# One operand sum of a Winograd-style matmul unit moved to a ScalarE negation and an adding DMA, with the products and the sums of h in another order (two-layer hybrid decoder trunk, 1 core)

## Chip, cores and metric

One core of one Trainium2 chip. The metric is the time of one execution in microseconds on the device; lower is better. Before the change three runs gave 2301.86, 2302.67 and 2303.2 us, median 2302.67 us.

## What is computed

A decoder trunk of two layers on 256 tokens of width 2048, everything in float32. Cut to its products, a layer is

```python
h = rms_norm(x, mix_norm[l])
z = h @ w_in[l]                                  # 2048 x 7168
a_out = chunked_spatial_gating(z[..., :c_a], ...)
b_out = dilated_attention(z[..., c_a:c_q], z[..., c_q:c_k], z[..., c_k:], ...)
mixed = concat(rms_norm(a_out), rms_norm(b_out))
x = x + mixed @ w_out[l]                         # 2048 x 2048
h = rms_norm(x, ffn_norm[l])
x = x + (silu(h @ w_gate[l]) * (h @ w_up[l])) @ w_down[l]   # 2048 x 5632, twice, and 5632 x 2048
```

The change concerns the last line, the FFN.

## The kernel before, in words

**Numbers.** Each float32 operand is split in two float32r halves, `hi` (a rounded copy, written by ScalarE) and `lo` (the rest, by a VectorE subtraction). A product is three matmuls, hi·hi, hi·lo and lo·hi (`mm3`, line 836). Weights arrive as raw tiles of 128 x 4 x 512 (1 MB) on SyncE's DMA queue and are split by `split_w`: ScalarE writes `wh`, then VectorE writes `wl = raw - wh`.

**Order.** The engines' queues are written out by hand. A list of items is walked; an item has a `prep` (load and split of its weights) and a `run` (its matmuls). Preps run ahead of runs by a ring of weight slots: 6 slots (`UNIT_RING`), two per item of four k-tiles, so the prep of item n+2 is issued just ahead of the run of item n. Other work, in generators called jobs, is issued between matmuls when a rough clock of each engine (`Queues`) says that it is due; `pause` and `Lease` belong to this planner. Nothing of the planner runs on the chip; it fixes the order in each queue, and semaphores do the rest.

**FFN stages.** In a layer the gate and up weights go by 11 column blocks j of 512, in chunks of 4, 4 and 3; after each chunk the down projection of that chunk follows, in two units (pairs of column blocks). One `unit` (line 871) multiplies the 256 tokens with two column blocks over some k-tiles by seven products instead of eight (the Strassen-Winograd form, `s` k-tiles per quarter: 4, or 2 in the last chunk's down units) and then adds plain products for the other k-tiles. Of the weights the quarters B11, B12, B22, B21 are loaded. `early` (line 890) makes e = B12 - B11 and overwrites B12 by B22 - B12, both on VectorE. `p1` makes B11 := B12 + B11 after splitting B11, `p2` makes B11 := B21 - B11 ahead of its split of B21. The items of a unit are, with the form of the activations that each takes: p1 (11), p5 (S1, weights e), p6 (S2, weights B11), p2 (12, weights B21), p7 (S3, weights B12), p3 (S4, weights B22), p4 (22, weights B11), then four plain items (`plains`). The runs r1 to r7 copy PSUM banks in between on ScalarE (after r1: X from bank 1; after r5: s5; after r6: Y from X; after r7: s3) and add s3 and s5 on VectorE after r3 and r4. `early` of the next unit stands behind the prep of the last plain item (five items earlier for the first unit).

**h.** At the end of a gate/up unit `gu_bank` (line 738) makes h on ScalarE and VectorE, pauses `H_NS` = 4000 ns of planner time and calls `put_h` (line 701): TensorE transposes, then for the first two blocks of a chunk the raw copy `xg` and, with the second, all seven forms by `make_forms` (line 619); for later blocks `quad_T` (line 258) splits straight into a plain table. The forms of the FFN input are made in the same way at the end of the attention stage (`put_f`), and the input of the next layer by `x_columns`.

Buffers of 8 KB per partition come from a pool of 22 (`SLOTS`).

Of the kernel before, what the change touches and what calls it, by code (L numbers as in the profile page):

```python
# [32 lines left out]
KC = 4  # L33
HK = 2
S_GU = 4
FORMS = ("11", "22", "S1", "S3", "S2", "12", "S4")

SLOTS = 22
PLAIN_RAW, PLAIN_RING = 3, 4
# [2 lines left out]

MM_NS = 227
FFN_LIMIT = 30000
H_NS = 4000
MARGIN_NS = 800
BACKLOG_NS = 4000
UNIT_NS = 3000
# [93 lines left out]
def trunk_kernel(ctx: ExitStack, tc: tile.TileContext, aps: dict):  # L142
# [21 lines left out]
    def slot(shape, dtype, name):  # L164

        return gen.tile(list(shape), dtype, tag="g", name=name)
# [33 lines left out]
    def pause(ns):  # L200
        q.chain = max(q.chain, q.pe) + ns
        yield


    class Job:
        def __init__(self, steps, limit):
# [48 lines left out]
                    identity=ident)  # L255
        return tp

    def quad_T(src_of, put, g_of, name, free=lambda: None):

        yield from sd_lease.take(2)  # L260
        both = slot([P, 2, 4, SEQ], F32R, name)
        hi, lo = both[:, 0], both[:, 1]
        tps = [transpose_pair(src_of, 2 * pr, name + "p") for pr in range(2)]
        free()
        yield
        for pr in range(2):
            tp = tps[pr]
            if g_of is None:
                sl = slice(2 * pr, 2 * pr + 2)
                act.activation(out=hi[:, sl, :], in_=tp, func=ACTF.Copy)  # L270
                dve.tensor_tensor(
                    out=lo[:, sl, :], in0=tp, in1=hi[:, sl, :].bitcast(F32), op=ALU.subtract)
            else:
                for i in range(2):
                    k = 2 * pr + i
                    split_scaled(hi[:, k, :], lo[:, k, :], tp[:, i, :], g_of(k))
            sd_lease.give()
            if pr == 0:
                yield
        put(hi, lo)  # L280

# [334 lines left out]
            sd_lease.give()  # L616
            yield

    def make_forms(F, xg):

        def quarter(t, h):
            return xg[:, h, :F.s, t * P:(t + 1) * P]
        a11, a12, a21, a22 = quarter(0, 0), quarter(0, 1), quarter(1, 0), quarter(1, 1)

        def split(f, src):
            hi, lo = F.at(f)
            act.activation(out=hi, in_=src, func=ACTF.Copy)
            dve.tensor_tensor(out=lo, in0=src, in1=hi.bitcast(F32), op=ALU.subtract)
            F.ready.add(f)
        split("11", a11)  # L630
        split("22", a22)
        dve.tensor_tensor(out=a22, in0=a21, in1=a22, op=ALU.add)
        dve.tensor_tensor(out=a21, in0=a11, in1=a21, op=ALU.subtract)
        yield
        split("S1", a22)
        split("12", a12)
        dve.tensor_tensor(out=a11, in0=a22, in1=a11, op=ALU.subtract)
        dve.tensor_tensor(out=a12, in0=a12, in1=a11, op=ALU.subtract)
        yield
        split("S2", a11)  # L640
        split("S3", a21)
        split("S4", a12)


    def x_columns(j, ssq, put, g_of, scale_done):
        cols = slice(j * W, (j + 1) * W)
        for t in range(NT):
            act.activation(
                out=junk, in_=xs[t][:, cols], func=ACTF.Square, accum_out=ssq[:, t, j:j + 1])
        yield from put(j, lambda t: xs[t][:, cols], lambda k: g_of(4 * j + k))  # L650
        if j == D // W - 1:
            scale_done()

    def put_plain(table, name):
# [4 lines left out]
    def put_f(L):  # L659

        plain = put_plain(L.fT, "fT")

        def put(j, src_of, g_of):
            if j >= 2:
                yield from plain(j, src_of, g_of)
                return
            if j == 0:
                L.xg = slot([P, 2, 4, SEQ], F32, "xg")
            yield from raw_T(src_of, L.xg[:, j], g_of, "fTp")
            if j == 1:  # L670
                L.f_halves = form_halves(8, "fF")
                L.fF = Forms(L.f_halves, S_GU)
                yield from make_forms(L.fF, L.xg)
        return put

    def wout_done(L, j, part):
# [17 lines left out]
    class Chunk:  # L694
# [4 lines left out]
            self.table, self.F, self.xg = {}, None, None  # L699

        def put_h(self, j, src_of, free):
            i = j - self.j0
            if i >= 2:
                yield from quad_T(
                    src_of, lambda hi, lo: self.table.__setitem__(i, (hi, lo)), None, "hT", free)
                return
            if i == 0:
                self.xg = slot([P, 2, 4, SEQ], F32, "xg")
            yield from raw_T(src_of, self.xg[:, i], None, "hTp", free)
            if i == 1:  # L710
                s = self.s
                if s < 4:
                    both = slot([P, 2, 2, 4 - s, SEQ], F32R, "hR")
                    rest = self.xg[:, :, s:, :]
                    for h in range(2):
                        act.activation(out=both[:, 0, h], in_=rest[:, h], func=ACTF.Copy)
                        dve.tensor_tensor(
                            out=both[:, 1, h], in0=rest[:, h], in1=both[:, 0, h].bitcast(F32),
                            op=ALU.subtract)
                    yield  # L720
                    flat = both.rearrange("p a h k t -> p a (h k) t")
                    self.table["r"] = (flat[:, 0], flat[:, 1])
                F = Forms(form_halves(6, "hF") + [self.L.f_halves[7]], s)
                self.F = F
                yield from make_forms(F, self.xg)

        def form(self, f, k):
            drain(lambda: self.F is not None)
# [9 lines left out]
    def gu_bank(L, j, chunk):  # L738

        s = {}  # L740

        def done(n, t, bank):
            if n == 0:
                yield lambda: hasattr(L, "r2")
                yield from t2_lease.take(1)
                s[t] = t2("s")
                act.activation(out=s[t], in_=bank, func=ACTF.Silu, scale=L.r2[:, t:t + 1])
                mm_lease.give()
                return
# [7 lines left out]
            yield from pause(H_NS)  # L757
            yield from chunk.put_h(j, lambda t: s[t], lambda: t2_lease.give(2))
        return done

# [110 lines left out]
    def unit(s, quarter, plains, form, done, lead=1):  # L871
# [16 lines left out]
            q.chain = saved  # L888

        def early():  # L890
            x11, x12, x22 = need(b11), need(b12), need(b22)
            U["e"] = slot([P, s, W], F32, "e")
            live[0] += 1
            w_sum(U["e"], x12, x11, ALU.subtract)
            w_sum(x12, x22, x12, ALU.subtract)

        def p1(it, parts=1):
            it.w = split_w(b11.tile)
            w_sum(b11.tile, b12.tile, b11.tile, ALU.add)

        def p5(it, parts=1):
            it.w = split_w(U["e"])
# [3 lines left out]
            it.w = split_w(b11.tile)  # L906

        def p2(it, parts=1):
            w_sum(b11.tile, need(b21), b11.tile, ALU.subtract)
            it.w = split_w(b21.tile)  # L910
            live[0] -= 1

        def p7(it, parts=1):
            it.w = split_w(b12.tile)
            live[0] -= 1

        def p3(it, parts=1):
            it.w = split_w(b22.tile)
# [37 lines left out]

        def r3(it):
            product(it, "S4", "Y", False)
            w_sum(bank["Z"], bank["Z"], U["s3"], ALU.add)

        def r4(it):
            product(it, "22", "X", False)
            w_sum(bank["Y"], bank["Y"], U["s5"], ALU.add)

        for p, r in ((p1, r1), (p5, r5), (p6, r6), (p2, r2), (p7, r7), (p3, r3), (p4, r4)):
            items.append(Item(1 if s <= 2 else 2, UNIT_RING, p, r))
        early_at[len(items) - 7 - lead] = early

        names = {(0, 0): "1", (1, 0): "Y", (0, 1): "X", (1, 1): "Z"}
        for i, (n, srcs, ops) in enumerate(plains):  # L970
            r = Raw(srcs, UNIT_RAW)
            raws.append(r)

            def prep(it, parts=1, r=r):
                it.w = split_w(need(r))
                live[0] -= 1

            def run(it, i=i, n=n, ops=ops):
                wh, wl = it.w
                for t in range(NT):  # L980
                    for k, op in enumerate(ops):
                        mm3(bank[names[n, t]], op(t), wh[:, k, :], wl[:, k, :], False, k == len(ops) - 1)
                        q.pe += 3 * MM_NS
                        run_jobs()
                    if i >= len(plains) - 2:
                        add(done(n, t, bank[names[n, t]]), FFN_LIMIT)
            items.append(Item(2, UNIT_RING, prep, run))

    for l, L in enumerate(layers):
        L.xss = const.tile([P, NT, 4], F32, name=f"xss{l}")  # L990
# [235 lines left out]
```

## Time and profile before

| | before |
|---|---|
| median of three runs | 2302.67 us |
| profiled execution | 2301.2 us |
| its span, first to last instruction | 2299.0 us |
| TensorE busy | 2261.3 us (98%) |
| VectorE busy | 1834.0 us (80%) |
| ScalarE busy | 1325.0 us (58%) |
| GpSimd busy | 52.4 us (2%) |
| DMA moved | 440.33 MB, mean 192 GB/s, 53.0% of 16 engines |

The page gives busy time, share of the span and instruction count of each engine. TensorE is busy nearly all of the time; the FFN stages of the two layers run from about 440 to 1145 us and from about 1585 us to the end, and there VectorE is busy for some nine tenths of the time. Line 90 is the helper through which all ScalarE and VectorE work is issued, so groups are told apart by tile names: `wh`, `wl`, `w` are split weights, `raw` and `e` weights, `C...` PSUM banks of a unit, `s` the halves of h and the saved s3 and s5, `hF` and `fF` forms, `hTp` transposes of h.

### The profile page before, as it was taken

The page shows a single profiled execution, that of the slowest core. Times are in us where ns is not written, and L with a number is a line of the kernel's source. Part 1 is how long each engine was busy: PE and PEld are TensorE (multiplying, and loading weights), DVE is VectorE, ACT ScalarE, POOL GpSimd, SP SyncE. Part 2 cuts the span into 40 slices and gives each one's busy share as a digit, 9 for nine tenths or more (in the row PEclk, how much of TensorE's full clock was granted, in tenths as well). Part 3 has the DMA queues.
Part 4 walks back from the last instruction along what each step waited for, and adds up shares of the span by engine and source line. Part 5 has one row for each costly group of instructions (what it writes and reads, how often), then busy time and mean ns, then how long its engine had stood idle before and what let it go on. Part 6 is the DMA issues. An engine that isn't in the chain of part 4 may idle for free.

```text
span 2299.0 us, 25930 instructions
## 1 busy us (share of the span) xinstructions
PE 2261.3 (98%) x10249; PEld 1864.1 (81%) x10249; DVE 1834.0 (80%) x1721; ACT 1325.0 (58%) x1590; POOL 52.4 (2%) x36
## 2 busy tenths in 40 slices
PE   9999999999999999999999999999999999999999
PEld 7888888878788878888788888887787888788887
DVE  6666766889999898998765666768899998989986
ACT  6455565565664665656555555646656556556563
POOL 0100000000000000000000001000000000000000
PEclk9999999999999999999999999999999999999999
DMA  9554455454465644745545444554545556447453
GB/s 361 176 183 165 165 175 204 174 198 165 183 237 183 224 179 159 264 181 201 183 174 193 164 165 165 183 212 173 183 165 198 223 186 235 165 165 274 165 201 110
DMA packets 66937, 440.33 MB, mean 192 GB/s; under 512 B 8064, under 2 KB 8576, under 8 KB 16768
## 3 DMA queue, kind: packets, MB, share of 16 engines
q1 hardware_dynamic: 66816, 438.69, 53.0%
q8 instruction: 80, 1.31, 0.2%
q14 instruction: 41, 0.34, 0.0%
HBM read 436.56 MB, written 2.10 MB: 191 GB/s over the span
## 4 chain that ended last, share of the span: by engine, by line
PE 77%; DVE 13%; issue 5%; ACT 3%; DMA 2%; SPq 0%; DVEq 0%; ACTq 0%
PE Z L836 30%; PE CX L836 15%; PE C L836 12%; PE CY L836 9%; PE CZ L836 8%; DVE wl L90 6%; ACT wh L90 2%; DVE raw L90 1%; PE sc L462 1%; DVE w L90 1%; DVE e L90 1%; PE hTp L253 1%; DMA gn<-in_k_norm 1%; PE qkp L253 1%; DVE hF L90 1%
## 5 line engine op out<-in xcount | busy, mean ns | idle before, releaser
L90 DVE TENSOR_TENSOR wl<-raw,wh 128x2048 fp32r<-128x2048 f32 x316 | 717.3, 2287 | 139.3 <-ACT wh L90 136.5
L90 ACT ACTIVATE wh<-raw 128x2048 fp32r<-128x2048 f32 x316 | 597.0, 1912 | 165.3 <-PE CX L836 56.3
L836 PE MATMUL Z<-w,xT 128*128 128x512 f32 x2688 | 641.5, 395 | 1.8 <-DVE xT L90 1.0
L836 PEld LDWEIGHTS Z<-w,xT 128*128 128x128 f32 x2688 | 499.2, 188 | 106.2 <-DVE w L90 1.6
L90 DVE TENSOR_TENSOR w<-raw,w 128x1024 fp32r<-128x1024 f32 (+1 forms) x313 | 376.9, 1217 | 214.8 <-ACT w L90 209.7
L90 ACT ACTIVATE w<-raw 128x1024 fp32r<-128x1024 f32 (+1 forms) x313 | 315.5, 1049 | 28.2 <-DMA raw<-in_w_in 9.1
L90 DVE TENSOR_TENSOR raw<-raw 128x2048 f32<-128x2048 f32 (+1 forms) x102 | 220.7, 2164 | 2.5
L836 PE MATMUL CX<-wh,fF 128*128 128x512 f32 x528 | 175.5, 391 | 1.5 <-ACT s L90 1.5
L836 PE MATMUL C<-wh,fF 128*128 128x512 f32 x352 | 118.7, 393 | 0.0
L836 PEld LDWEIGHTS CX<-wh,fF 128*128 128x128 f32 x528 | 99.1, 188 | 23.5 <-ACT s L90 2.4
L836 PE MATMUL CY<-wh,fT 128*128 128x512 f32 x352 | 115.9, 390 | 0.4
L836 PE MATMUL C<-wh,fT 128*128 128x512 f32 x352 | 115.6, 389 | 0.0
L836 PE MATMUL CZ<-wh,fT 128*128 128x512 f32 x352 | 115.5, 389 | 0.0
L836 PE MATMUL CX<-wh,fT 128*128 128x512 f32 x352 | 115.5, 389 | 0.0
L836 PE MATMUL CX<-wl,fF 128*128 128x512 f32 x264 | 102.7, 389 | 0.0
L90 ACT ACTIVATE CX<-C 128x512 f32<-128x512 f32 x34 | 19.8, 582 | 125.0 <-PE C L836 125.0
L836 PE MATMUL Z<-w,bT 128*128 128x512 f32 x384 | 89.9, 391 | 0.0
L836 PE MATMUL Z<-w,aT 128*128 128x512 f32 x384 | 89.1, 390 | 0.0
L836 PEld LDWEIGHTS Z<-w,aT 128*128 128x128 f32 x384 | 71.8, 188 | 14.8
L836 PEld LDWEIGHTS Z<-w,bT 128*128 128x128 f32 x384 | 71.8, 188 | 14.7
L836 PE MATMUL CY<-wh,fF 128*128 128x512 f32 x240 | 78.9, 390 | 0.0
L836 PEld LDWEIGHTS CY<-wh,fT 128*128 128x128 f32 x352 | 66.1, 188 | 15.6 <-issue 2.0
(191 smaller groups left out, 3445.0 us busy)
## 6 DMA issues: line engine op xcount, KB each, us to landing
raw<-in_w_in SPq DMA_DIRECT2D x109, 1024.0 KB, 4.8
raw<-in_w_gate SPq DMA_DIRECT2D x88, 1024.0 KB, 4.8
raw<-in_w_up SPq DMA_DIRECT2D x88, 1024.0 KB, 4.9
raw<-in_w_down SPq DMA_DIRECT2D x72, 1024.0 KB, 4.9
raw<-in_w_out SPq DMA_DIRECT2D x32, 1024.0 KB, 4.8
raw<-in_w_down SPq DMA_DIRECT2D x32, 512.0 KB, 4.6
raw<-in_w_in SPq DMA_DIRECT2D x5, 512.0 KB, 8.1
xstage<-in_xT SPq DMA_DIRECT2D x8, 256.0 KB, 7.4
```

Source lines behind the costliest of these rows:

```text
L90: return f(**kw)
L253: nc.tensor.transpose(out=tp[:, i, t * P:(t + 1) * P], in_=src_of(t)[:, (c0 + i) * P:(c0 + i + 1) * P], identity=ident)
L462: nc.tensor.matmul(out=sc[:, g, :n], lhsT=L.kv[pair, g][:, h, t * P:(t + 1) * P], rhs=kT[:, h, :n], start=True, stop=True)
L836: nc.tensor.matmul(out=out, lhsT=a, rhs=b, start=start and n == 0, stop=stop and n == 2, skip_group_check=True)
```

## The change

`early` keeps e on VectorE. B12 is negated in place on ScalarE, and a DMA from GpSimd's queue reads B22 a second time from HBM and adds it into B12. `p1` makes its sum from B22 and e instead of from B12; the sum of `p2` moves to `p7`, behind its split. In units of s = 4 the items come as p1, p5, p6, p2, p3, p7, plain 1, p4, plain 0, plain 2, plain 3, in those of s = 2 as p1, p5, p6, p2, plain 1, p7, p3, plain 3, p4, plain 0, plain 2; s5 and s3 are added after the first and second half of the plain item behind p7 or p3. The forms come in the order of use, in two generators: 11 and S3 as soon as the first column block is there, the rest with the second. `put_h` is placed by planned TensorE time: transposes 7.0 us after the job starts, what follows at 13.5 us and in steps of 4.5 us (1.5 and 3.0 us for the last block of the last chunk).

```diff
-FORMS = ("11", "22", "S1", "S3", "S2", "12", "S4")
+FORMS = ("11", "S3", "S1", "22", "S2", "12", "S4")
-H_NS = 4000
+T_NS, H_NS, STEP_NS = 7000, 13500, 4500
+LAST_T_NS, LAST_H_NS = 1500, 3000
+    def until(pe):
+        q.chain = q.pe - MARGIN_NS
+        yield lambda: q.pe >= pe
+        q.chain = q.pe
...
+    def first_forms(F, xg):
+        a11, a12, a21, a22 = quarters(F, xg)
+        form(F, "11", a11)
+        dve.tensor_tensor(out=a11, in0=a11, in1=a21, op=ALU.subtract)
+        form(F, "S3", a11)
+
+    def other_forms(F, xg, at=None):
+        a11, a12, a21, a22 = quarters(F, xg)
+        form(F, "22", a22)
+        dve.tensor_tensor(out=a21, in0=a21, in1=a22, op=ALU.add)
+        dve.tensor_tensor(out=a22, in0=a22, in1=a11, op=ALU.subtract)
         yield
+        if at is not None:
+            yield from until(at + STEP_NS)
+        form(F, "S1", a21)
+        form(F, "12", a12)
+        dve.tensor_tensor(out=a12, in0=a12, in1=a22, op=ALU.subtract)
         yield
+        if at is not None:
+            yield from until(at + 2 * STEP_NS)
+        form(F, "S2", a22)
+        form(F, "S4", a12)
...
         def put_h(self, j, src_of, free):
-            i = j - self.j0
+            i, end = j - self.j0, q.pe
+            last = i == self.n - 1 and self.n < 4
+            at = end + (LAST_H_NS if last else H_NS)
+            yield from until(end + (LAST_T_NS if last else T_NS))
...
         def early():
-            x11, x12, x22 = need(b11), need(b12), need(b22)
+            x11, x12 = need(b11), need(b12)
+            need(b22)
             U["e"] = slot([P, s, W], F32, "e")
             live[0] += 1
             w_sum(U["e"], x12, x11, ALU.subtract)
-            w_sum(x12, x22, x12, ALU.subtract)
+            saved, q.chain = q.chain, q.pe
+            act.activation(out=x12, in_=x12, func=ACTF.Copy, scale=-1.0)
+            q.chain = saved
+            nc.gpsimd.dma_start(
+                out=x12, in_=quarter(1, 1), accum_op=ALU.add, max_dma_last_dim=2 * W)
         def p1(it, parts=1):
             it.w = split_w(b11.tile)
-            w_sum(b11.tile, b12.tile, b11.tile, ALU.add)
+            w_sum(b11.tile, b22.tile, U["e"], ALU.subtract)
         def p2(it, parts=1):
-            w_sum(b11.tile, need(b21), b11.tile, ALU.subtract)
-            it.w = split_w(b21.tile)
-            live[0] -= 1
+            it.w = split_w(need(b21))
         def p7(it, parts=1):
             it.w = split_w(b12.tile)
-            live[0] -= 1
+            w_sum(b11.tile, b21.tile, b11.tile, ALU.subtract)
+            live[0] -= 2
...
+        products((p1, r1), (p5, r5), (p6, r6), (p2, r2))
+        if s == 4:
+            products((p3, r3), (p7, r7))
+            plain(1, add_s5, add_s3)
+            products((p4, r4))
+            plain(0)
+            plain(2)
+            plain(3)
+        else:
+            plain(1)
+            products((p7, r7), (p3, r3))
+            plain(3, add_s5, add_s3)
+            products((p4, r4))
+            plain(0)
+            plain(2)
```

## Rows read from the trace of the kernel before

**Rows 1.** The page, its first line.
```profile
span 2299.0 us, 25930 instructions
```
**Rows 2.** Windows over both FFN stages: each engine's busy us (instructions), clock, DMA share, GB/s.
```profile
440.00:1145.00 705.00, 687.51 (x3061) 564.24 (x3060) 619.00 (x391) 416.35 (x349) 0.69 (x1) 1.00 0.54 197
1585.00:2287.00 702.00, 688.47 (x3066) 565.63 (x3065) 616.97 (x385) 411.95 (x333) 0.70 (x1) 1.00 0.53 192
```
**Rows 3.** The chain that ended last, one piece: start us, us, what.
```profile
472.13 2.72 PE CX L836 x12
```
**Rows 4.** TensorE's waits, whole run: who waited for whom, us, times, longest.
```profile
PE C L836 <- DVE wl L90: 12.7, 14, 1.2
PE CZ L836 <- DVE s L90: 5.4, 4, 1.4
PE CX L836 <- ACT s L90: 4.0, 3, 2.5
PE CZ L836 <- DVE xs L90: 2.5, 2, 1.2
```
**Rows 5.** TensorE's waits, 1080 to 1145 us (last down units of layer 0).
```profile
PE CX L836 <- ACT s L90: 2.5, 1, 2.5
PE CX L836 <- ACT CY L90: 1.6, 2, 1.1
PE C L836 <- DVE hT L90: 1.2, 1, 1.2
```
**Rows 6.** The page, costliest groups: count | busy us, mean ns | idle before.
```profile
L90 DVE TENSOR_TENSOR raw<-raw 128x2048 f32<-128x2048 f32 (+1 forms) x102 | 220.7, 2164 | 2.5
```
**Rows 7.** Timeline, VectorE, around unit j = 5: start, us, what, [idle before <-releaser].
```profile
730.53 2.29 DVE L90 TENSOR_TENSOR e<-raw 128x2048 f32<-128x2048 f32 x1
732.85 2.29 DVE L90 TENSOR_TENSOR raw<-raw 128x2048 f32<-128x2048 f32 x1
...
755.87 4.50 DVE L90 TENSOR_TENSOR wl<-raw,wh 128x2048 fp32r<-128x2048 f32 x2 [0.43 <-ACT wh L90]
```
**Rows 8.** Timeline, ScalarE, the same unit.
```profile
737.12 0.69 ACT L90 ACTIVATE s<-C,r 128x512 f32<-128x512 f32 x1 [9.42 <-PE C L836]
...
753.44 0.58 ACT L90 ACTIVATE CY<-CX 128x512 f32<-128x512 f32 x1 [0.32 <-PE CX L836]
753.93 3.71 ACT L90 ACTIVATE wh<-raw 128x2048 fp32r<-128x2048 f32 x2
```
**Rows 9.** Timeline, TensorE, the same unit: start of r2, transposes, start of r7.
```profile
753.24 0.39 PE L836 MATMUL C<-wh,fF 128*128 128x512 f32 x1
...
755.28 1.03 PE L253 MATMUL hTp<-ident,s 128*128 128x128 f32 x8
...
756.85 0.39 PE L836 MATMUL CX<-wh,fF 128*128 128x512 f32 x1
```
**Rows 10.** Timeline, TensorE and VectorE, start of unit j = 3.
```profile
567.07 1.29 DVE L90 TENSOR_TENSOR hF<-xg,hF 128x512 fp32r<-128x512 f32 x2
...
578.14 0.74 DVE L90 SCALAR_TENSOR_TENSOR s<-CY,r,s 128x512 f32<-128x512 f32 x1
579.03 0.47 PE L836 MATMUL CZ<-wh,fF 128*128 128x512 f32 x1 [1.35 <-DVE s L90]
581.66 2.28 DVE L90 TENSOR_TENSOR raw<-raw 128x2048 f32<-128x2048 f32 x1
...
584.57 0.39 PE L836 MATMUL C<-wh,fF 128*128 128x512 f32 x1
586.20 0.50 PE L836 MATMUL C<-wl,fF 128*128 128x512 f32 x1 [1.24 <-DVE wl L90]
...
586.54 0.62 PE L836 MATMUL C<-wh,fF 128*128 128x512 f32 x2
```
**Rows 11.** DMA issues: out<-in, queue, count, KB each, median us to landing.
```profile
raw<-in_w_gate SPq DMA_DIRECT2D x88, 1024.0 KB, 4.8
xs<-in_x SPq DMA_DIRECT2D x2, 1024.0 KB, 13.8
```

More of the change, by code (lines that the diff above doesn't have):

```diff
@@ L256, in transpose_pair, with quad_T @@
         return tp
-    def quad_T(src_of, put, g_of, name, free=lambda: None):
+    def quad_T(src_of, put, g_of, name, free=lambda: None, at=None):
         yield from sd_lease.take(2)
-        both = slot([P, 2, 4, SEQ], F32R, name)
-        hi, lo = both[:, 0], both[:, 1]
         tps = [transpose_pair(src_of, 2 * pr, name + "p") for pr in range(2)]
@@ L265, in quad_T @@
         yield
+        if at is not None:
+            yield from until(at)
+        both = slot([P, 2, 4, SEQ], F32R, name)
+        hi, lo = both[:, 0], both[:, 1]
         for pr in range(2):
@@ L277, in quad_T @@
             sd_lease.give()
-            if pr == 0:
+            if pr == 0 and at is None:
                 yield
@@ L617, in raw_T, with quarters, form, x_columns @@
             yield
[L619 to L633, printed above, removed]
-        yield
[L635 to L638, printed above, removed]
-        yield
[L640 to L645, printed above, removed]
+    def quarters(F, xg):
+        return [xg[:, h, :F.s, t * P:(t + 1) * P] for t in range(NT) for h in range(2)]
+    def form(F, f, src):
+        hi, lo = F.at(f)
+        act.activation(out=hi, in_=src, func=ACTF.Copy)
+        dve.tensor_tensor(out=lo, in0=src, in1=hi.bitcast(F32), op=ALU.subtract)
+        F.ready.add(f)
+    def first_forms(F, xg):
[8 more added lines that the diff above has]
+        dve.tensor_tensor(out=a22, in0=a22, in1=a11, op=ALU.subtract)
+        yield
+        if at is not None:
[3 more added lines that the diff above has]
+        dve.tensor_tensor(out=a12, in0=a12, in1=a22, op=ALU.subtract)
+        yield
+        if at is not None:
+            yield from until(at + 2 * STEP_NS)
+        form(F, "S2", a22)
+        form(F, "S4", a12)
+    def x_columns(j, ssq, put, g_of, scale_done, done=set()):
         cols = slice(j * W, (j + 1) * W)
@@ L650, in x_columns @@
         yield from put(j, lambda t: xs[t][:, cols], lambda k: g_of(4 * j + k))
-        if j == D // W - 1:
+        done.add(j)
+        if len(done) == D // W:
+            done.clear()
             scale_done()
@@ L669, in put @@
             yield from raw_T(src_of, L.xg[:, j], g_of, "fTp")
-            if j == 1:
+            if j == 0:
                 L.f_halves = form_halves(8, "fF")
-                L.fF = Forms(L.f_halves, S_GU)
-                yield from make_forms(L.fF, L.xg)
+                F = Forms(L.f_halves, S_GU)
+                first_forms(F, L.xg)
+                L.fF = F
+            else:
+                yield from other_forms(L.fF, L.xg)
         return put
@@ L701, in put_h @@
         def put_h(self, j, src_of, free):
-            i = j - self.j0
+            i, end = j - self.j0, q.pe
+            last = i == self.n - 1 and self.n < 4
+            at = end + (LAST_H_NS if last else H_NS)
+            yield from until(end + (LAST_T_NS if last else T_NS))
             if i >= 2:
                 yield from quad_T(
-                    src_of, lambda hi, lo: self.table.__setitem__(i, (hi, lo)), None, "hT", free)
+                    src_of, lambda hi, lo: self.table.__setitem__(i, (hi, lo)), None, "hT", free, at)
                 return
@@ L709, in put_h @@
             yield from raw_T(src_of, self.xg[:, i], None, "hTp", free)
[L710 to L725, printed above, removed]
+            yield from until(at)
+            if i == 0:
+                self.F = Forms(form_halves(6, "hF") + [self.L.f_halves[7]], self.s)
+                first_forms(self.F, self.xg)
+                return
+            s = self.s
+            if s < 4:
+                both = slot([P, 2, 2, 4 - s, SEQ], F32R, "hR")
+                rest = self.xg[:, :, s:, :]
+                for h in range(2):
+                    act.activation(out=both[:, 0, h], in_=rest[:, h], func=ACTF.Copy)
+                    dve.tensor_tensor(
+                        out=both[:, 1, h], in0=rest[:, h], in1=both[:, 0, h].bitcast(F32),
+                        op=ALU.subtract)
+                yield
+                flat = both.rearrange("p a h k t -> p a (h k) t")
+                self.table["r"] = (flat[:, 0], flat[:, 1])
+            yield from other_forms(self.F, self.xg, at)
         def form(self, f, k):
@@ L756, in done @@
                 return
-            yield from pause(H_NS)
             yield from chunk.put_h(j, lambda t: s[t], lambda: t2_lease.give(2))
@@ L958, in r3, with add_s3, add_s5, plain @@
             product(it, "S4", "Y", False)
-            w_sum(bank["Z"], bank["Z"], U["s3"], ALU.add)
         def r4(it):
             product(it, "22", "X", False)
+        def add_s3():
+            w_sum(bank["Z"], bank["Z"], U["s3"], ALU.add)
+        def add_s5():
             w_sum(bank["Y"], bank["Y"], U["s5"], ALU.add)
[L965 to L970, printed above, removed]
+        def plain(i, mid=lambda: None, end=lambda: None):
+            n, srcs, ops = plains[i]
             r = Raw(srcs, UNIT_RAW)
             raws.append(r)
-            def prep(it, parts=1, r=r):
+            def prep(it, parts=1):
                 it.w = split_w(need(r))
                 live[0] -= 1
-            def run(it, i=i, n=n, ops=ops):
+            def run(it):
                 wh, wl = it.w
@@ L984, in run, with products @@
                         run_jobs()
-                    if i >= len(plains) - 2:
+                    (mid, end)[t]()
+                    if i >= 2:
                         add(done(n, t, bank[names[n, t]]), FFN_LIMIT)
             items.append(Item(2, UNIT_RING, prep, run))
+        def products(*pairs):
+            for p, r in pairs:
+                items.append(Item(1 if s <= 2 else 2, UNIT_RING, p, r))
+        names = {(0, 0): "1", (1, 0): "Y", (0, 1): "X", (1, 1): "Z"}
+        early_at[len(items) - lead] = early
+        products((p1, r1), (p5, r5), (p6, r6), (p2, r2))
[6 more added lines that the diff above has]
+            plain(3)
+        else:
+            plain(1)
[4 more added lines that the diff above has]
+            plain(2)
     for l, L in enumerate(layers):
```

## The prediction

> **What bounds the kernel now.** I read the views in this order: the page, the windows of the two FFN stages, TensorE's waits, and the timelines of two units. The profiled execution took 2301.2 us, its span is 2299.0 [rows 1], so 2.2 us lie outside it; the median of the runs is 1.5 us above it, and I add the change to the median. In the FFN windows TensorE is busy for 687.5 of 705 us and 688.5 of 702 us [rows 2]: 17.5 and 13.5, together 31.0 us idle. Twelve matmuls in a row take 2.72 us [rows 3], or 0.227 us each, and the change leaves their number alone. So the kernel is bound by TensorE, and what an order can give back is its waits. VectorE is the other busy engine there (619 and 617 us, 88%), ScalarE is not (416 and 412 us) [rows 2].
>
> A wait costs more than its row. At 586.20 the row says 1.24 us idle [rows 10], but that matmul starts 1.63 us after the one before, 1.40 above the pitch, and the next starts 0.34 after it, 0.11 above the pitch. So I take the idle time plus 0.27 us a wait.
>
> The waits fall in four places. (a) r2 waits for the `wl` of p2: it is the row at 586.20, and the row of VectorE at 581.66 shows why, for the sum B21 - B11 goes ahead of the split [rows 10]. Of 14 waits, 12.7 us, of that kind [rows 4] two, 0.9 each, stand at plain items; 12 waits and 10.9 us remain, in the last unit of a chunk of four and the two down units behind it. (b) r5 waits for a bank that the `s` product on VectorE frees: 4 times, 5.4 us [rows 4], the row at 579.03, with the product at 578.14 queued late [rows 10]. (c) The short products of the last down units wait for ScalarE's copies and for h: 5.3 us in layer 0 [rows 5]; layer 1 idles 4.0 us less than layer 0 [rows 2], which I put down to this place, so 1.3 there. (d) The remaining 31.0 - 10.9 - 5.4 - 6.6 = 8.1 us stand mainly in the first unit of each layer, j = 0, such as the waits for `xs` [rows 4].
>
> **The change, part by part.**
>
> *VectorE loses one sum per unit, 34 in all.* `raw<-raw` counts 102, three in each of 34 units, at 2164 ns [rows 6]. So 34 x 2.16, some 70 us, leave VectorE, and as it is no bound by itself, they count only where TensorE waits for it.
>
> *p2 loses its sum.* With no sum ahead of it, p2's split follows ScalarE's `wh`, and h no longer comes in between. I take (a) as gone: 10.9 + 12 x 0.27 = 14.2 us gained (bounds 9 and 14.2).
>
> *The negation and its wait.* ScalarE must wait for e, since e reads B12; queued behind the negation are p1's `wh` and the silu. VectorE then waits for that `wh`: from the end of e 1.91 us for the negation (I price it like a `wh` of the same size, 3.71 for two, a pitch of 1.8 to 1.9 [rows 8]) and 1.91 for `wh`, 3.8 us idle in place of the 2.2 us sum. In an ordinary unit this is covered: ScalarE itself stands idle 9.4 us there [rows 8]. It is not where VectorE is full, in the unit that makes eight operations of forms (0.65 each [rows 10], 5.2 us). I add VectorE's queue up there from r2's 8.2 us after the unit's start: p7's `wl` starts at 10.8 (below), then eight operations of 2.2, ten small ones, 6.6 us, e ends at 35.0; the negation 37.0, `wh` 38.8, p1's `wl`, its sum and p5's `wl` to 45.5, the `s` product 46.2. The next unit starts at 41.8 and its r5 at 44.5, so it waits 1.8 us, 1.9 with the restart, 4 times: 7.6 us. The waits under (b), 5.4 + 4 x 0.27 = 6.5, are replaced by this: 1.1 lost (bounds 6.5 gained, 6 lost).
>
> *The moved sum.* It now stands between p7's split and plain 1's. In r2 of the unit at 745 us, ScalarE's copy to Y, after r6, starts at 753.44, the `wh` behind it at 753.93, its `wl` at 755.87 and the next VectorE operation 2.21 later [rows 7, 8]. In the new order that `wh` is p7's, and behind its `wl` come the sum and plain 1's `wl`: it ends at 755.87 + 2.21 + 2.20 + 2.29 = 762.57. r2 starts at 753.24 [rows 9], three products of 2.72 later plain 1 starts, and its second matmul needs `wl` at 761.63: 1.0 late, 1.1 with the restart. Where h is transposed in r2, TensorE itself is later by 756.85 - 753.24 - 2.72 = 0.89 [rows 9], and 0.1 late remains, 0.2 with the restart. Eight units (j = 4, j = 8 and two second down units a layer) have no transposes, 20 have: 8 x 1.1 + 20 x 0.2 = 12.8 us lost (bounds 5 and 31).
>
> *The adding DMA.* GpSimd issues it once the negation is done; its queue held one instruction in each FFN window [rows 2], so nothing queues behind it. p7's `wh` waits for it, at 753.93, and behind that stand all of ScalarE's copies. e ended at 732.8 [rows 7], so the negation would end at 734.8: 19 us are there, 13 in the full units. No row shows an adding DMA or one from GpSimd. The nearest, a plain load of 1 MB, lands in 4.8 us, and one beside a crowded start in 13.8 [rows 11]; I take the range from those, nearer the first, and nothing for it. 30 units of 1 MB and 4 of 0.5 add 34 MB, 8%, to DMA engines that are 54% busy [rows 2], so I take nothing for later weight loads (bound 5 us). SyncE's queue is moved in one way: B21 gives its buffer back with p7 in place of p2, so the load that waits for it starts two items, 5.4 us, later; the plain items that it feeds come two products later or more, so I take nothing (inside the same bound). The Trainium skill (DMA: Bandwidth & Descriptors, Anatomy of one DMA) gives about 2.0 us plus the bytes at 436 GB/s for a DMA from GpSimd, and Collectives: The Full Stack says that a reduction reads two sources and runs at half the rate; by both, an estimate of 7 us, the sum would be the same.
>
> *Last down units.* A plain item now stands between r2 and r7 and between r3 and r4, so the copies have 5.4 us. h must be there two items earlier, at 13.6 us after the start, and is transposed at some 4 us. (c) is 6.6 us in five or six waits, 8.1 with restarts; I leave 1.5 a layer for new ones, as `p7` is prepared early and may wait for its DMA: 5.1 gained (bounds 0 and 8).
>
> *First units and the layer change.* Under (d) the wait for `xs` (2 x 1.2 [rows 4]) goes with the VectorE sum ahead of it; the splits of the FFN input still sit between ScalarE's copies, and plain 1 waits as above. 8.1 + 8 x 0.27 is 10.3; I leave 7, 3.3 gained (bounds 4 lost, 7 gained). At the end of layer 0 the third block of x comes last and is wanted four k-tiles, 5.4 us, sooner: 0.5 lost (bounds 0 and 2.5).
>
> Sum: 14.2 - 1.1 - 12.8 + 5.1 + 3.3 - 0.5 = 8.2 us gained; 2301.2 - 8.2 = 2293.0 against the profiled execution, 2294.5 against the median.
>
> **The rivals.**
>
> *Nothing takes the waits' place.* VectorE has 4.4 us less ahead of p2; if plain 1's split and r5 find it free, the 7.6 and 12.8 us above are not paid: 2294.5 - 20 = 2274. For it: the units j = 5 and 6 have no wait today. Against: the copy to Y fixes p7's `wh`, and three VectorE operations behind it last 6.7 us [rows 7].
>
> *The moved sum delays every plain 1.* If the transposes come too early or late to cover it, 28 units pay 1.1, 18 more than above: 2312. Against: planned at 7 us behind the job's start, about 9 behind the unit's, they fall in r2.
>
> *The adding DMA lands late.* It decides from 19 us behind the negation, 13 in full units. Each us beyond it, less about 0.7 of slack before r7, is paid in 30 units: at 21 us some 39 us, 2333, and more above. For it: two streams of loads share the engines, and the crowded load of 13.8 us [rows 11] is at the edge. The Trainium skill (SBUF — State Buffer, Who interferes with whom) has a rule that speaks this way: VectorE operations in a two-port mode keep GpSimd from writing descriptors; it names copies and `tensor_scalar`, not `tensor_tensor`, and nearly all VectorE rows here are TENSOR_TENSOR [rows 6, 7].
>
> *The change does not do what it says:* the waits under (a) follow another input, ScalarE's `wh` behind the copy, and stay: 2294.5 + 9 = 2303, the same.
>
> **How the numbers follow.** A measurement of this kernel can tell some 0.2%, 4.6 us, from no change: faster is below 2298.1, slower above 2307.3. Chances: forecast 0.50, its own range 2284 to 2304, of which 0.37 faster and 0.13 the same; nothing in their place 0.22, faster; every plain 1 0.12, of which 0.04 the same and 0.08 slower; late DMA 0.10, slower; waits stay 0.06, the same. Faster 0.59, same 0.23, slower 0.18. The range for 8 in 10 takes in both ends but for the late DMA: 2274 to 2313.
>
> **What would show it.** Right: no wait of r2 for `wl`; waits of about 1 us on `C... <- DVE wl` or `CY <- DVE wl` at plain 1 of units without transposes; r5 of j = 3 and 7 waiting for `s`; 68 `raw<-raw`; VectorE idle 3.8 us behind e with ScalarE named; the adding DMA landing 5 to 14 us after issue. Wrong: ScalarE's p7 `wh` released by a DMA; weight loads landing later than their splits; a TensorE pitch other than 0.227 us.

## The result and the profile after

The changed kernel takes 2319.50 us (median of 4 runs, 2317.86 to 2320.44) against 2302.64 for the kernel before: a ratio of 1.0073, 95% interval 1.0055 to 1.009. It is slower by 16.9 us, where 8.2 us of gain were forecast, and above the top of the range, 2313. The profiled execution took 2319.54 us.

The page of the changed kernel: its first line, the new group of ScalarE, two DMA queues (packets, MB, share of 16 engines), and issues (count, KB each, median us to landing).

```profile
span 2317.8 us, 26042 instructions
...
L91 ACT ACTIVATE raw<-raw 128x2048 f32<-128x2048 f32 (+1 forms) x34 | 61.8, 1817 | 209.5 <-DVE e L91 209.5
...
q1 hardware_dynamic: 66816, 438.69, 52.0%
q0 software_dynamic: 33312, 33.56, 9.3%
...
raw<-in_w_up SPq DMA_DIRECT2D x88, 1024.0 KB, 6.4
raw<-in_w_up POOLq DMA_DIRECT2D x22, 1024.0 KB, 8.9
raw<-in_w_down POOLq DMA_DIRECT2D x8, 1024.0 KB, 10.2
```

The change does what it says: 34 negations, all waiting for e, and 34 adding DMAs. The span grew by 18.8 us [rows 1]. The windows of the two FFN stages, with the columns of [rows 2]:

```profile
440.00:1153.00 713.00, 694.38 (x3063) 566.32 (x3063) 585.26 (x376) 442.24 (x362) 24.90 (x17) 0.99 0.67 215
1595.00:2300.00 705.00, 687.23 (x3032) 560.51 (x3031) 579.84 (x366) 436.97 (x347) 24.90 (x17) 1.00 0.66 213
```

VectorE is relieved, by 34 and 37 us, the 70 of the forecast, and ScalarE has 25 to 26 us more. But TensorE idles 18.6 and 17.8 us, 36.4 in place of 31.0 [rows 2], and in the first window its clock is no longer 1.00. TensorE's waits over the whole run, beside [rows 4]:

```profile
PE CY L863 <- DVE wl L91: 10.4, 10, 1.8
PE CZ L863 <- DVE s L91: 5.4, 4, 1.4
PE CY L863 <- ACT CY L91: 4.2, 1, 4.2
PE hTp L260 <- DVE s L91: 3.8, 2, 1.9
PE CX L863 <- ACT CX L91: 3.5, 1, 3.5
PE CY L863 <- ACT wh L91: 3.2, 2, 1.6
PE CZ L863 <- DVE xs L91: 2.7, 7, 0.4
...
PE C L863 <- DVE xs L91: 1.5, 4, 0.4
PE C L863 <- DVE wl L91: 1.4, 4, 0.4
```

The 14 waits of `C` for `wl` have shrunk to 4 of 0.3 to 0.4 us, and the 5.4 us for `s` stand as they were. New or grown are plain 1 (`CY`, for `wl` and `wh`; before two waits, 1.8 us), the many short ones for `xs`, most of them at the start of the second down units, and the long waits of the last down units.

**Where they come from.** The timelines of ScalarE, VectorE and TensorE at the start of j = 3 (the stretch of [rows 10]):

```profile
569.49 1.92 ACT L91 ACTIVATE raw<-raw 128x2048 f32<-128x2048 f32 x1 [6.08 <-DVE e L91]
571.31 1.90 ACT L91 ACTIVATE wh<-raw 128x2048 fp32r<-128x2048 f32 x1
...
567.18 2.28 DVE L91 TENSOR_TENSOR e<-raw 128x2048 f32<-128x2048 f32 x1
573.24 2.29 DVE L91 TENSOR_TENSOR wl<-raw,wh 128x2048 fp32r<-128x2048 f32 x1 [3.78 <-ACT wh L91]
...
582.08 0.47 PE L863 MATMUL CZ<-wh,fF 128*128 128x512 f32 x1 [1.36 <-DVE s L91]
```

ScalarE waits for e, negates, then writes p1's `wh`; VectorE stands idle for 3.78 us until that `wh` is there. It has lost a sum of 2.2 us and gained a hole of 3.8. In the second down units the same hole stands ahead of the additions to `xs`, which free the banks of the unit before:

```profile
658.55 2.29 DVE L91 TENSOR_TENSOR wl<-raw,wh 128x2048 fp32r<-128x2048 f32 x1 [3.78 <-ACT wh L91]
...
663.09 0.68 DVE L91 TENSOR_TENSOR xs<-C,xs 128x512 f32<-128x512 f32 x1
...
663.91 0.47 PE L863 MATMUL C<-wh,hF 128*128 128x512 f32 x1 [0.37 <-DVE xs L91]
```

The moved sum B21 - B11 stands between the `wl` of p7 and that of plain 1, VectorE first, then TensorE:

```profile
675.51 2.29 DVE L91 TENSOR_TENSOR wl<-raw,wh 128x2048 fp32r<-128x2048 f32 x1 [0.43 <-ACT wh L91]
677.72 2.29 DVE L91 TENSOR_TENSOR raw<-raw 128x2048 f32<-128x2048 f32 x1
679.92 6.74 DVE L91 TENSOR_TENSOR wl<-raw,wh 128x2048 fp32r<-128x2048 f32 x3
...
682.26 0.50 PE L863 MATMUL CY<-wl,hT 128*128 128x512 f32 x1 [0.84 <-DVE wl L91]
```

In the first unit of a layer more hangs on that sum. The splits of the FFN input go to and fro between VectorE and ScalarE, and plain 1's `wh` stands behind them in ScalarE's queue:

```profile
459.64 2.29 DVE L91 TENSOR_TENSOR raw<-raw 128x2048 f32<-128x2048 f32 x1
461.85 0.48 DVE L91 SCALAR_TENSOR_TENSOR fT<-fTp,ffng,fT 128x256 fp32r<-128x256 f32 x1
...
462.36 0.47 ACT L91 ACTIVATE fT<-fTp,ffng 128x256 fp32r<-128x256 f32 x1 [4.60 <-DVE fT L91]
462.73 3.70 ACT L91 ACTIVATE wh<-raw 128x2048 fp32r<-128x2048 f32 x2
...
464.69 0.49 PE L863 MATMUL CY<-wh,fT 128*128 128x512 f32 x1 [1.59 <-ACT wh L91]
467.01 0.68 PE L863 MATMUL CY<-wl,fT 128*128 128x512 f32 x1 [1.83 <-DVE wl L91]
```

In the last down units waits of three kinds are long: in both layers the transposes of h wait for the product that they read (1.92 us; layer 0 is shown), in layer 0 a product waits for a copy that stands on ScalarE behind the splits of the next `xT`, and in layer 1 one waits for a copy behind a `wh` whose load is late:

```profile
1094.55 1.16 PE L260 MATMUL hTp<-ident,s 128*128 128x128 f32 x7 [1.92 <-DVE s L91]
...
1133.11 0.47 ACT L91 ACTIVATE xT<-xTp,mixg 128x256 fp32r<-128x256 f32 x1 [3.80 <-DVE xT L91]
...
1134.91 0.60 ACT L91 ACTIVATE CY<-CX 128x512 f32<-128x512 f32 x1
1135.56 0.50 PE L863 MATMUL CY<-wh,hR 128*128 128x512 f32 x1 [4.25 <-ACT CY L91]
...
2282.30 1.91 ACT L91 ACTIVATE wh<-raw 128x2048 fp32r<-128x2048 f32 x1 [5.35 <-DMA raw<-in_w_down]
...
2284.75 0.96 PE L863 MATMUL CX<-w,hF 128*128 128x512 f32 x3 [3.54 <-ACT CX L91]
```

### The profile page after: what moved, and what is told of

It is laid out like the page before. It is cut to its first block, busy times and chain, and to the rows that moved or that the text cites. A ratio compares the mean times of both kernels' runs of the same rounds, so it can differ in the third digit from the quotient of the medians.

```text
span 2317.8 us, 26042 instructions
## 1 busy us (share of the span) xinstructions
PE 2272.9 (98%) x10249; PEld 1866.3 (81%) x10249; DVE 1763.1 (76%) x1687; ACT 1379.1 (60%) x1624; POOL 104.3 (5%) x70
## 3 DMA queue, kind: packets, MB, share of 16 engines
q1 hardware_dynamic: 66816, 438.69, 52.0%
q0 software_dynamic: 33312, 33.56, 9.3%
## 4 chain that ended last, share of the span: by engine, by line
PE 82%; DVE 9%; ACT 4%; issue 3%; DMA 2%; SPq 0%; DVEq 0%; ACTq 0%
PE Z L863 30%; PE CX L863 16%; PE C L863 12%; PE CZ L863 11%; PE CY L863 10%; DVE wl L91 4%; ACT wh L91 2%; DVE raw L91 2%; PE sc L471 1%; DVE w L91 1%; DMA gn<-in_k_norm 1%; PE hTp L260 1%; ACT w L91 1%; DVE xs L91 1%; DVE e L91 1%
## 5 line engine op out<-in xcount | busy, mean ns | idle before, releaser
L91 ACT ACTIVATE w<-raw 128x1024 fp32r<-128x1024 f32 (+1 forms) x313 | 316.1, 1049 | 14.4 <-DMA raw<-in_w_in 8.8
L91 ACT ACTIVATE raw<-raw 128x2048 f32<-128x2048 f32 (+1 forms) x34 | 61.8, 1817 | 209.5 <-DVE e L91 209.5
L863 PE MATMUL CY<-wl,fT 128*128 128x512 f32 x176 | 72.7, 413 | 7.0 <-DVE wl L91 7.0
## 6 DMA issues: line engine op xcount, KB each, us to landing
raw<-in_w_down POOLq DMA_DIRECT2D x8, 1024.0 KB, 10.2
```

What stands on the lines that cost most here:

```text
L91: return f(**kw)
L863: nc.tensor.matmul(out=out, lhsT=a, rhs=b, start=start and n == 0, stop=stop and n == 2, skip_group_check=True)
```

## The experiments

The theory after the result is that the slowdown is made by two places in in-order queues, the negation ahead of p1's split on ScalarE and the sum between p7's and plain 1's splits on VectorE. The rivals are the adding DMA with its traffic, and the new order of products itself. The experiments set the two places apart and together; the kernel before ran beside all of them (medians 2302.27 to 2302.52).

**B22 - B12 on VectorE again**, all else changed: no negation, no adding DMA.

```diff
...
-            act.activation(out=x12, in_=x12, func=ACTF.Copy, scale=-1.0)
...
-            nc.gpsimd.dma_start(out=x12, in_=quarter(1, 1), accum_op=ALU.add, ...)
+            w_sum(x12, b22.tile, x12, ALU.subtract)
```

> The changed kernel with B22 - B12 made by VectorE again (no negation, no adding DMA), order and timing of the rest as changed. If the wait of VectorE for ScalarE behind the negation makes the waits of r5 in j = 3 and 7 (4 x 1.6 us) and at the start of the second down units (4 x 1.3 us): those 11.5 us go, about 2308 us (2305 to 2312), and the waits of 1.0 us at plain 1 stay. If the adding DMA itself (33.6 MB more, loads of w_up landing in 6.4 instead of 4.8 us) costs the 17 us: about 2302. If neither: 2319, or above, as VectorE has 2.2 us more in each unit.

2303.53 us, ratio 1.0005 (0.9995 to 1.0014): below the 2305 to 2312 expected, and near the 2302 of the rival, so that this run alone does not part the negation from its DMA; the fourth experiment does. The negation with its DMA costs 16.0 us where the change puts it, although it takes 70 us of work from VectorE. The waits for `s` at j = 3 and 7 are gone with it, those of plain 1 (10.4 us, 10 times) stay.

**The negation alone, in the kernel before**, at the same place; p1's sum is then B22 - e.

```diff
...
-            w_sum(x12, x22, x12, ALU.subtract)
...
+            act.activation(out=x12, in_=x12, func=ACTF.Copy, scale=-1.0)
...
+            nc.gpsimd.dma_start(out=x12, in_=quarter(1, 1), accum_op=ALU.add, ...)
...
-            w_sum(b11.tile, b12.tile, b11.tile, ALU.add)
+            w_sum(b11.tile, b22.tile, U["e"], ALU.subtract)
```

> The kernel before with the negation, the adding DMA and B11's sum from e alone; items, moved sum, forms and h timing as before. If the negation costs only at starts of units: r5 of j = 3 and 7 and the starts of second down units wait, r2 still waits, 2303 to 2312 us, no wait at plain items and no further spells of the lower TensorE clock. If the adding DMA is the cost: about 2319. If it is harmless: 2302, or less by what VectorE saves.

2310.67 us, 1.0034 (1.0021 to 1.0047): slower in the old order too, by 8.3. r2 waits as expected, and r5 of j = 3 and 7 a little longer than before (1.6 against 1.35 us). Other things were not expected: the second down units' starts do not wait, but the first unit of each layer waits 2.9 us for `xs` (before 1.2), and the lower clock comes oftener: the profiled execution, the slowest of the five at 2313.27 us and 0.996, has four stretches at half clock more than the kernel before, behind waits of 2.0 and 2.9 us.

**The sum later still**, behind the split of plain 1 (in the short units, behind p7's, where the change has it); `last_sum` is the moved line.

```diff
         def p7(it, parts=1):
             it.w = split_w(b12.tile)
-            w_sum(b11.tile, b21.tile, b11.tile, ALU.subtract)
...
             def prep(it, parts=1):
                 it.w = split_w(need(r))
+                if s == 4 and i == 1:
+                    last_sum()
```

> The changed kernel with the sum B21 - B11 put behind the split of plain 1 instead of ahead of it (units of s = 4 only). If that place is what costs: the 8 waits of 1.1 us at plain 1, the 20 of 0.2, the two of some 4 us at plain 1 of j = 0 (whose fT splits stand behind the sum) and the spells of lower clock behind these (about 5 us) go, together 20 to 25 us: 2295 to 2300 us. If the waits only move to the next item, p4: 2315 to 2320.

2341.51 us, 1.017 (1.0154 to 1.0185): a gain of 20 to 24 us on the change was expected, and 22 were lost. Its waits of TensorE, and ScalarE's timeline:

```profile
PE CX L863 <- ACT s L91: 13.2, 8, 2.4
PE CZ L863 <- DVE s L91: 12.7, 4, 3.2
...
603.44 1.92 ACT L91 ACTIVATE wh<-raw 128x2048 fp32r<-128x2048 f32 x1 [5.02 <-DVE raw L91]
```

The product behind plain 1, p4, is the sum's reader. Its `wh` now waits 5.02 us for the sum, and behind that `wh` stand ScalarE's copy to s3 and the splits that follow. The sum has to go earlier, not later.

**The negation behind p1's split**, all else changed; `negate` holds the negation and its DMA, taken out of `early`.

```diff
         def p1(it, parts=1):
             it.w = split_w(b11.tile)
+            negate()
             w_sum(b11.tile, b22.tile, U["e"], ALU.subtract)
```

> The changed kernel with the negation and the adding DMA behind the split of p1 in ScalarE's queue, so that VectorE doesn't wait through it. If VectorE's 3.8 us idle behind e makes the waits of r5 and at the start of second down units: 11.5 us less, about 2308 us. The adding DMA then starts some 2 us later, and p7's split has less time: if that is too little, ScalarE's wh waits for the DMA and the time is 2320 or above.

2302.26 us, 1.0003 (0.9993 to 1.0012): 17.2 us come back, more than the 11 expected. The waits for `s` and nearly all for `xs` are gone (0.4 us left); plain 1's stay. The adding DMA is still there 34 times, so it is not what made the 16.0 us.

**The sum ahead of p2's split again**, all else changed, the negation at its early place.

```diff
         def p2(it, parts=1):
-            it.w = split_w(need(b21))
+            w_sum(b11.tile, need(b21), b11.tile, ALU.subtract)
+            it.w = split_w(b21.tile)
...
         def p7(it, parts=1):
             it.w = split_w(b12.tile)
-            w_sum(b11.tile, b21.tile, b11.tile, ALU.subtract)
...
```

> The changed kernel with the sum B21 - B11 ahead of p2's split again, as before, all else as changed. If the sum's place between p7 and plain 1 costs: the 8 waits of 1.1 us and the 20 of 0.2 at plain 1, the two of 3.9 us at plain 1 of j = 0 and the spells of lower clock right behind those two (some 5 us) go, and r2 waits for its wl where VectorE is late (six units, up to 1.5 us each): 2319.5 - 25 + 5, about 2300 us. If VectorE is simply full, so that the sum delays something wherever it stands: 2312 to 2320.

2302.48 us, 1.0001 (0.9992 to 1.001): 17.0 us come back. r2's waits return in full,

```profile
PE C L863 <- DVE wl L91: 15.8, 16, 1.2
```

and yet it is faster: as those return, the four waits for `s`, plain 1's go but for 1.5 us in the first unit of each layer, and the transposes wait 1.6 us for h in place of 3.8. The clock's mean is 0.998 in place of 0.996, some 4 of the 17 us.

**Both moves together**, the negation behind p1's split and the sum ahead of p2's (the last two edits).

> The changed kernel with the sum ahead of p2's split and the negation with its DMA behind p1's split. If the two places are the whole cost and independent: 2302.3 of the negation moved alone, less some 18 to 22 us: 2281 to 2285. If VectorE is full: 2295 to 2302.

2279.54 us, 0.9901 (0.9885 to 0.9918), a little below the 2281 to 2285 expected. Its longest waits of TensorE:

```profile
PE C L863 <- DVE wl L91: 3.1, 4, 0.8
PE CY L863 <- DVE wl L91: 3.0, 2, 1.5
```

With VectorE kept busy behind e, the sum ahead of p2's split makes only 3.1 us of waits, though it stands where it stood in the kernel before.

**The later negation alone, in the kernel before** (the second experiment with the negation behind p1's split).

> The kernel before with the negation and the adding DMA alone, but behind p1's split. With them ahead of it the kernel before became 8.3 us slower; if that was VectorE's 3.8 us idle behind e, the 8 us go and the 2.2 us that VectorE saves in each unit come through: 2290 to 2300 us. If the adding DMA has a cost of its own: 2303 to 2311.

2287.85 us, 0.9939 (0.9924 to 0.9954): 14.7 us below the kernel before, 22.8 below the early negation, and below the 2290 to 2300 expected. The adding DMA, there 34 times in both, is not free: in the short units of this kernel ScalarE's splits wait for it four times, 12.7 us in all,

```profile
ACT w L90 <- DMA raw<-in_w_down: 12.7, 4, 8.1
```

and in the unit of the wait of 8.1 us TensorE waits 2.0 us for a copy of ScalarE's (1.1 at that place before); whether the DMA makes that is not shown.

**The new order alone**: the sum at p2, B22 - B12 on VectorE (the first and the fifth edit together).

> The changed kernel with both disputed steps taken out: B22 - B12 is the one VectorE operation of the kernel before (no negation, no adding DMA), and the sum B21 - B11 goes back to its place ahead of p2's split. What is left of the change is the new order of products, the plain tiles and the timing of the sums of h. If the slowdown is made by the two steps alone, 2285 to 2290 us: the kernel before less what the order takes away (12 to 17 us), as a kernel with the negation in its later place on top of it gave 2279.5. If the new order itself loses time at plain 1 of the first unit and at the last down units, and the gain of the other kernel came from the freed VectorE, 2298 to 2305 us.

2284.96 us, 0.9923 (0.9907 to 0.994). The new order of products, with its plain tiles between the copies and the planned sums of h, is worth 17 us by itself, and which part of it makes them was not taken apart; its waits of `C` for `wl` are

```profile
PE C L863 <- DVE wl L91: 7.1, 8, 1.0
```

So the medians of nine kernels stand in a table, us:

| order; place of B21 - B11 | B22 - B12 on VectorE | negation ahead of p1's split | negation behind it |
|---|---|---|---|
| new; behind p7's split | 2303.5 | 2319.5 (the change) | 2302.3 |
| new; ahead of p2's split | 2285.0 | 2302.5 | 2279.5 |
| old; ahead of p2's split | 2302.3 to 2302.6 (before) | 2310.7 | 2287.9 |

Down the columns, the moved sum costs 18.6, 17.0 and 22.7 us. Along the rows, the early negation costs 16.0, 17.5 and 8.3, the later one gains 1.3 (inside the spread of the runs), 5.4 and 14.7. Neither rival of the theory stands as the cause of the slowdown: the DMA is in the right column too, and the new order gains. What the DMA costs apart from the work that it takes from VectorE was not measured.

**The sums of h in the last down units later**, on top of both steps: transposes due 4.0 us after the job's start in place of 1.5, the rest at 5.5 in place of 3.0.

```diff
-LAST_T_NS, LAST_H_NS = 1500, 3000
+LAST_T_NS, LAST_H_NS = 4000, 5500
```

> The changed kernel with both moved (sum ahead of p2's split, negation behind p1's split) and with the last block's h transposed at 4.0 instead of 1.5 us behind the job's start, split at 5.5 instead of 3.0. If the two waits of the transposes for the s product (1.9 us, with the half clock behind one of them) come from transposes that are queued too early: 4 to 6 us below the kernel without this last edit, 2276 to 2280 us. If h then comes too late for plain 3: no gain or a loss.

2278.44 us, 0.9896 (0.9881 to 0.991). The waits of the transposes for h are gone from TensorE's list; the intervals with and without this edit overlap, so its 1.1 us are not settled.

**The output's stores on GpSimd's queue**, on top of that. (Its expectation calls the last sums of h due earlier; they are due at 4.0 and 5.5 us, which is later, as above. And the negation stands behind p1's split, not plain 1's.)

```diff
-                nc.sync.dma_start(out=aps["out"][t * P:(t + 1) * P, cols], in_=xs[t][:, cols])
+                nc.gpsimd.dma_start(out=aps["out"][t * P:(t + 1) * P, cols], in_=xs[t][:, cols])
```

> The changed kernel with the negation behind plain 1's split, the sum B21 - B11 ahead of p2's split and the last down units' sums of h due 4.0 and 5.5 us earlier, and with the stores of the output issued from GpSimd's queue in place of SyncE's, where they wait for VectorE and stand ahead of the raw loads of w_down. If those loads are late because of the stores in front of them, the wait of TensorE's copy of 2.8 to 3.5 us near the end of layer 1 goes: 2275 us against 2278.4 without this. If they are late for their buffers, or the stores now stand in front of the adding DMA instead, 2278 to 2281 us.

2275.43 us (2274.66 to 2275.84), 0.9883 (0.9868 to 0.9898). Near the end, of the kernel without this edit: SyncE's queue, ScalarE's timeline and TensorE's waits (2200 us on):

```profile
2222.75 8.11 SPq L798 DMA_DIRECT2D out<-xs  x2
2230.95 2.66 SPq L823 DMA_DIRECT2D raw<-in_w_down  x3
...
2239.03 1.91 ACT L91 ACTIVATE wh<-raw 128x2048 fp32r<-128x2048 f32 x1 [7.05 <-DMA raw<-in_w_down]
...
PE CX L863 <- ACT CX L91: 3.1, 1, 3.1
```

The load for which that `wh` waits is the second of the three, issued at 2231.43, behind two stores that hold the queue from 2222.75 on. With this edit, SyncE's queue and ScalarE's only wait of `w` or `wh` for a DMA there:

```profile
2222.23 14.09 SPq L823 DMA_DIRECT2D raw<-in_w_down  x6
...
ACT w L91 <- DMA raw<-in_w_down: 1.1, 1, 1.1
```

The same load is now issued at 2222.60, some 9 us earlier: the stores held the loads back, and without them in front the wait of 3.1 us on TensorE is gone. The 1.1 us left are for an adding DMA (issued at 2229.77), behind which no wait of TensorE above 0.7 us follows there. All four runs lie below all four without the edit, but the two intervals overlap, so that the size of the 3.0 us is not settled. This version beats both kernels: 1.2% below the kernel before, 1.9% below the change.

## Why the prediction was wrong, step by step

Measured in the trace of the changed kernel, an excess is the time from one matmul's start to the next beyond 0.227 us (0.109 for a transpose), summed over the rows of a place of the FFN stages, of both layers, and taken against the same sum in the kernel before. What matmuls take longer at half clock is kept apart.

| step of the sum | predicted, us | measured, us |
|---|---|---|
| r2's waits (a) | -14.2 | -14.4 |
| negation: r5 of j = 3, 7 (b) | +1.1 | 0.0 |
| moved sum at plain 1 | +12.8 | +12.8 (8 of 1.1, 20 of 0.2) |
| a later plain item of j = 1, 5 | none | +2.5 |
| start of second down units | none | +5.2 |
| last down units (c) | -5.1 | +5.2 |
| first units (d) | -3.3 | -1.0 |
| layer change | +0.5 | 0.0 (no wait of TensorE from 1136 to 1602 us) |
| clock | none | +6.3 |
| all other rows, none above 0.3 | none | +1.2 |
| sum | -8.2 | +17.8 (the span: +18.8; 0.9 of it lies outside the FFN stages) |

**What was right.** r2's waits went, plain 1's came, of the size and in the eight units that the prediction named (the row at 682.26: 0.84 idle, 1.1 with the restart; forecast 1.1). r5 of j = 3 and 7 waits 1.36, 1.6 with the restart, against 1.9. VectorE is idle 3.78 us behind e, as worked out (3.8). The adding DMA lands 5.9 to 12.7 us after its issue (34 rows of GpSimd's queue), and no split on ScalarE was released by it in the changed kernel: the rival of a late DMA fell, and so did the rival that every plain 1 is delayed.

**What failed, first: the last down units.** The prediction took the long waits as covered by the plain items put in between and left 1.5 us a layer. There are 13.7 us in the two layers, in new places, where 5.1 were to be gained and 5.2 were lost. The transposes are queued 1.5 us after the job's start, ahead of the product that they read: 1.92 us twice. In layer 0 a copy on ScalarE stands behind the ping-pong of the next `xT` splits (4.2 us), in layer 1 behind a `wh` whose load, issued at 2276.35, is late behind a store (3.5). Here nothing was worked out from a queue; a place where all engines are at work was given a round number.

**Second: the negation was charged at one place only.** The 3.8 us hole on VectorE was priced at r5, and r5 alone; what is queued behind it in the second down units, `xs`, was not gone through: 5.2 us. And the waits (b) were taken as replaced by the negation's. The new order without the negation has none of them: they did not have to be replaced, they were kept by it.

**Third: the first units.** That the splits of the input sit between ScalarE's copies stood in the prediction; that the moved sum delays them, and through them plain 1's `wh`, did not. These are waits of 1.6 + 1.8 us a layer, and 1.0 us was gained where 3.3 were put.

**Fourth: the clock.** Its mean over the run is 0.996, before 0.999: 0.004 x 2317.8 = 9.3 us lost against 2.3, to the rounding of these means; by the rows of the FFN stages the difference is 6.3. The sum had no term for it.

**The deepest one: (a) was credited to the wrong step.** The gain (a) was booked on the sum's removal from p2, so that its cost at plain 1, well forecast, seemed paid for. With the sum at p2, the new order alone has 7.1 us of those waits, and with the negation later 3.1: most of (a) comes from the order and from a VectorE that isn't held up, and the sum never had to move. Where VectorE is this busy, a wait taken from r2 comes out at r5, at plain 1 or at h: the kernel with the sum at p2 and the negation early, set beside the change, shows the swap.

Taken step by step through the table of nine, the order gains 17 us. The prediction had 14.4 that go with it: 6.5 of (b), 5.1 of (c) and 3.3 of (d), less 0.5. The moved sum loses 18.6 on top of that, 6 to 7 of them by the clock (0.996 for 0.999); the prediction had 1.4 gained, 14.2 less 12.8. The early negation loses 16.0 on top of both, where the prediction had 7.6. So by these runs it was the two moves that were priced wrong, by 20 and by 8 us, and not the adding of steps: by time the sum and the early negation add up almost exactly, 2285.0 + 18.6 + 17.5 = 2321.1 against 2319.5 (with the later negation the sum costs 4 us more).

## What to carry to other kernels

An operation that is taken off a busy engine pays only if the wait that it brings is shorter than the operation: 2.2 us of VectorE's work were given for 3.8 us of waiting, until the negation was put behind the next operation that VectorE waits for. Before an operation is moved in an in-order queue, name its next reader and everything queued behind that reader, at each kind of unit and not only at the fullest; both places right next to it can be wrong, one for what follows it in its own queue and one for its reader. And a gain should be credited to a step only after asking whether another step of the same change takes it anyway.

## What the runs showed of the hardware

**The clock behind waits.** The first unit of layer 1, in the changed kernel (a short stretch and a long one) and in the kernel before (columns of [rows 2]):

```profile
1621.60:1627.60 6.00, 6.00 (x14) 4.71 (x15) 5.42 (x7) 3.29 (x4) 0.00 (x0) 0.50 0.48 175
1600.00:1650.00 50.00, 46.18 (x193) 37.17 (x192) 37.93 (x26) 29.61 (x27) 2.29 (x2) 0.93 0.62 194
```
```profile
1590.00:1640.00 50.00, 46.20 (x204) 36.84 (x203) 42.34 (x30) 29.82 (x28) 0.70 (x1) 1.00 0.50 184
```

The granted clock fell to half, 1.2 GHz, for a part of it, during and right behind the waits of plain 1; the row at 467.01 above (0.68 us, where matmuls behind other waits took 0.47 to 0.50) shows the same in layer 0. In the FFN stages of the changed kernel this came with waits of 1.6 + 1.8, 1.9 and 4.2 us, but not with each: the second 1.92 us and the 3.5 us of layer 1 were followed by none. The kernel before has one such stretch there, at its wait of 2.5 us [rows 5]. So a wait of that size can cost more than itself. The new order has 0.996 with the sum behind p7's split and 0.999 with it at p2 (B22 - B12 on VectorE in both).

**The adding DMA.** 1 MB landed after 8.9 us (w_up) and 10.2 (w_down), median, where a plain load of 1 MB takes 4.8 [rows 11]. The estimate of 7 us by two pages of the Trainium skill (DMA: Bandwidth & Descriptors, Anatomy of one DMA; Collectives: The Full Stack, The bandwidth ceiling: the fold count and why AG ≠ RS ≠ AR) is below both; the measurement decides. Its 33.56 MB kept the 16 engines for 9.3% of the span and the 438.69 MB of the other queue for 52.0%: 0.28 against 0.12% per MB, 2.3 times as much.

**What made later weight loads late.** w_up's loads land after 6.4 us in the changed kernel, 4.9 before. It goes with the moved sum rather than with the adding DMA: with the sum back at p2 they land after 4.9 us with the DMA, and with the sum moved after 5.9 us without it. Both have a share in w_down's 1 MB loads: 6.1 us in the changed kernel, 5.0 with the sum moved and no DMA, 4.9 with the DMA and the sum at p2. The prediction had one part of this, the load that waits for B21's buffer and starts later, and took nothing for it; that holds for w_up, for no split on ScalarE waits for one of its loads. Its sign of being wrong, a load that lands later than its split wants it, did show once: the `wh` at 2282.30, which waits 5.35 us for a load of w_down behind a store.
